# Issue order on ScalarE and VectorE in a two-layer hybrid block with eight routed experts

## The chip, the cores and the metric

The kernel runs on one core of a Trainium2 chip. The metric is device time in microseconds (us), median of several executions. TensorE (PE, its weight loads PEld), VectorE (DVE), ScalarE (ACT), GpSimd (POOL) and SyncE (SP) run side by side. Each takes its own instructions in the order in which the program was scheduled and waits on semaphores for the others. All weights are read from HBM by DMAs that SP issues.

## The reference

256 tokens of width 1024 go through two layers. A layer is a mixer (dilated attention, stick-breaking attention, a causal convolution, three gates, an output product) and a feed-forward part: a dense SwiGLU in layer 0, a routed one in layer 1. The change is in the routed one:

```python
logits = einsum(t, w_router) + b_router
top_logits, top_idx = lax.top_k(logits, 2)
gates = softmax(top_logits)
for each expert e, for the tokens routed to it:
    a = xb @ w_exp_gate[e]                  # 1024 x 2816
    u = xb @ w_exp_up[e]                    # 1024 x 2816
    y = (silu(a) * u) @ w_exp_down[e]       # 2816 x 1024
out[token] += gate * y
```

## The kernel before

**Precision.** Products run as pairs of fp32r operands: a value is `hi` (the value rounded by a ScalarE copy, L288) and `lo` (the rest, a VectorE subtraction, L292). A full expert does three products per weight tile (hi·hi, lo·hi, hi·lo).

**Experts.** The eight experts run in the order of `RANKS`, called E0 to E7 here. E0, E1, E3 and E5 are full (128 token slots, three products). E2, E4, E6 and E7 are short: 64 slots, the hi and lo halves of the tokens side by side in one stationary tile, so two products per weight tile, and a fold (L1198) of the lower half onto the upper after ScalarE has copied it out (`low`, L1195). In a short expert every fifth load (`WHOLE`) is not split: PE multiplies the raw fp32 tile. Each expert has 34 loads (E7 35), of 1 MB but for two (E7 four) of half that: 33 MB.

**The stream of weights.** `_Stream` makes units in order. `_make` issues the load of a unit into one of 9 load buffers (5 of `raw`, `MORE_BUFS` = 4 of `more`) and emits its `hi` and its `lo`, each into one of 8 part buffers, so that four split units fit. `next` hands out unit n and first fills the stream while no more than three split units wait (`AHEAD_E`): in the text of the program the split of unit n+3 stands ahead of the products of unit n.

**Stages of an expert.** Gate and up products by columns of 512 (`project_e`), two units each. At the end of a gate product ScalarE takes `silu` (`ea`, L1225); at the end of an up product VectorE multiplies (L1228). `turn` transposes the result on PE (`eaT`) and splits it into an `ehl` tile of the `slab` pool (4 KB per partition each, 8 of them; the gathered tokens `xg` take four of the pool for each pair of experts). Then the down products into two banks; `y_half` splits each half into `yhi` and `ylo`, and `scatter` multiplies by the transposed selection, ScalarE scales by the gate (`add`, L1155) and POOL adds into `x` (L1156). The last expert uses one VectorE instruction (L1158) in place of these two. Between the two experts of a pair (p odd) `gather` brings in the tokens of the next pair: four `piece`s, one to a tick, each two PSUM banks that ScalarE copies out (L1106).

**Ticks.** `tick()` runs after each unit's products. `later(n, fn)` puts `fn` n ticks on, so that small work goes between units.

**What sets the order.** The tile framework schedules each engine's instructions in an order of its own, from dependencies, the order in the text as priority, and its own estimate of when operands will be ready. `_InOrder` wraps an engine (`act_`, `dve_`) and ties each instruction behind the engine's previous one in the text. Before the change only the routing ahead of the experts uses these wrappers; in the experts ACT and DVE stand in the scheduler's order.

Of the kernel before, what the change touches and what calls it, by code (L numbers as in the profile page):

```python
# [7 lines left out]
F32 = mybir.dt.float32  # L8
# [25 lines left out]
RAW_BUFS = 5  # L34
PART_BUFS = 4
SLABS = 17
MORE_BUFS = 4
MORE_PARTS = 4
AHEAD = 3 * 1024
AHEAD_E = 3 * 2048  # L40
WARM = 7
MOE_SLABS = 8
UNIT_E = 2048
SHORT = P // 2

# [179 lines left out]
class _Stream:  # L225
# [3 lines left out]
    def __init__(self, tc, raw_pool, part_pool, ahead):  # L229
        self.tc = tc  # L230
        self.nc = tc.nc
        self.raw_pool = raw_pool
        self.part_pool = part_pool
        self.ahead = ahead
        self.plan = []
        self.units = []
        self.raws = {}
        self.more_pool = None
        self.more_parts = None
        self.hold = None  # L240
        self.lo_late = None
        self.turn = -1
        self.part_turn = -1
        self.made = 0
        self.waiting = 0

    def raw_tile(self, shape):

# [20 lines left out]
    def _make(self):  # L269
        nc = self.nc  # L270
        key, ci, u, ku, n, whole = self.units[self.made]
        size = ku * n
        self.made += 1
        src, length = self.plan[ci]
        if ci not in self.raws:
            raw = self.raw_tile([P, length])
            nc.sync.dma_start(raw, src() if callable(src) else src)
            self.raws = {ci: raw}
        part = self.raws[ci][:, u * size:(u + 1) * size]
        if whole:  # L280
            return key, 0, part.rearrange("p (k n) -> p k n", n=n), None
        self.waiting += size
        if 2 * size <= UNIT_E:
            both = self.part_tile("hilo")
            hi, lo = both[:, :size], both[:, size:2 * size]
        else:
            hi, lo = (self.part_tile(q)[:, :size] for q in ("hi", "lo"))
        ins = nc.scalar.activation(hi, part, AF.Copy)  # L288
        if self.lo_late is not None:
            self.tc.keep_in_program_order(ins)  # L290
        if self.lo_late is None:
            nc.vector.tensor_tensor(lo, part, hi.bitcast(F32), op=ALU.subtract)  # L292
        else:
            self.lo_late.append(lambda e: e.tensor_tensor(lo, part, hi.bitcast(F32), op=ALU.subtract))
        return (key, size, hi.rearrange("p (k n) -> p k n", n=n), lo.rearrange("p (k n) -> p k n", n=n))
# [34 lines left out]
def tile_kernel(ctx, tc, x, weights, experts, columns, consts, gains, out, dbg=None):  # L330
# [48 lines left out]
    for t in range(TT):  # L379
        nc.sync.dma_start(xs[t], x[0, t * P:(t + 1) * P, :])  # L380
    nc.scalar.dma_start(cols[:, :R_TAP], columns[:, :R_TAP])
    ident = con[:, C_ID:C_ID + P]
    ones = con[:, C_ONE:C_ONE + P]
    trir = cst.tile([P, P], F32R, name="trir")
# [653 lines left out]
        rt["slots"].append(sl)  # L1038

    def moe():  # L1040
        hhi, hlo, rs2, sels, picks, slots = (rt[k] for k in ("hi", "lo", "rs2", "sels", "picks", "slots"))

        low_1 = lambda e: low(1)
# [23 lines left out]
        def gather(pair, slots, at_once=False, late=()):  # L1067
# [25 lines left out]
            def piece(kp):  # L1093
                xg.append(T([P, 2, 2 * width], "xg", F32R))
                for j in range(2):
                    k = 2 * kp + j
                    b = ax_bank("xgp")
                    for q, src in enumerate((hhi, hlo)):
                        for t in range(TT):
                            pe.matmul(b[:, q * width:(q + 1) * width], src[:, t, k * P:(k + 1) * P],  # L1100
                                      slots_of[q][:, t], start=t == 0, stop=t == TT - 1)
                    to, of = xg[kp][:, j, :], b[:, :2 * width]
                    if both:
                        to = to.rearrange("p (i q s) -> p q i s", i=2, q=2)
                        of = of.rearrange("p (q i s) -> p q i s", i=2, q=2)
                    act.activation(to, of, AF.Copy)  # L1106

            pts, rss = [], []
            for fn in late:
# [35 lines left out]

        def scatter(gate, last, pt, yhi, ylo, h):
            sl = slice(h * 512, (h + 1) * 512)
            for t in range(TT):
                b = ax_bank("sc")
                pe.matmul(b, pt[:, t * P:(t + 1) * P], yhi[:, sl], start=True, stop=False)  # L1150
                pe.matmul(b, pt[:, t * P:(t + 1) * P], ylo[:, sl], start=False, stop=True)
                g = gate(t)
                if not last:
                    add = work.tile([P, 512], F32, tag="add", name="add", bufs=2)
                    act.activation(add, b, AF.Copy, scale=g)  # L1155
                    pool.tensor_tensor(xs[t][:, sl], xs[t][:, sl], add, op=ALU.add)  # L1156
                else:
                    dve.scalar_tensor_tensor(xs[t][:, sl], b, g, xs[t][:, sl], op0=ALU.mult, op1=ALU.add)  # L1158
            if last:
                later(1 if h else 4, lambda: store(sl))  # L1160

        def store(sl):
            for t in range(TT):
# [2 lines left out]
        def expert(i, short, part, pts, rss, gate, last, beside):  # L1166
# [74 lines left out]
            def y_half(h, bank):  # L1241
                sl = slice(h * 512, (h + 1) * 512)
                split_evac(yhi[:, sl], ylo[:, sl], bank)
                scatter(gate, last, pts[i], yhi, ylo, h)

            bk = [None, None]
            k_h = [0, 0]
# [163 lines left out]
```

## Time and profile before

| what | value |
|---|---|
| median of 3 executions | 1553.1 us (1551.66 to 1553.54) |
| profiled execution, its own time | 1553.46 us |
| its span in the trace | 1551.7 us |
| PE / PEld / DVE / ACT busy | 95% / 72% / 73% / 62% |
| granted TensorE clock | 0.989 |
| bytes moved by DMA | 400.17 MB |

The experts take from about 754 us to the end. The trace counts PE as busy while matmuls overlap, with modelled ends, so that a busy PE is not PE at its peak; the number of matmuls in a stretch and what they waited for tell more. "Idle before" of an engine names what released it.

### The profile page before, as it was taken

The page shows a single profiled execution, that of the slowest core. Times are in us where ns is not written, and L with a number is a line of the kernel's source. Part 1 is how long each engine was busy: PE and PEld are TensorE (multiplying, and loading weights), DVE is VectorE, ACT ScalarE, POOL GpSimd, SP SyncE. Part 2 cuts the span into 40 slices and gives each one's busy share as a digit, 9 for nine tenths or more (in the row PEclk, how much of TensorE's full clock was granted, in tenths as well). Part 3 has the DMA queues.
Part 4 walks back from the last instruction along what each step waited for, and adds up shares of the span by engine and source line. Part 5 has one row for each costly group of instructions (what it writes and reads, how often), then busy time and mean ns, then how long its engine had stood idle before and what let it go on. Part 6 is the DMA issues. An engine that isn't in the chain of part 4 may idle for free.

```text
span 1551.7 us, 17848 instructions
## 1 busy us (share of the span) xinstructions
PE 1480.0 (95%) x6596; PEld 1124.5 (72%) x6596; DVE 1132.7 (73%) x1233; ACT 967.5 (62%) x1039; POOL 92.8 (6%) x69
## 2 busy tenths in 40 slices
PE   9989999999999989999999999999998999989887
PEld 7867787788888777787888887557774577755554
DVE  5898657555547797666899887678875788677665
ACT  6646653544435656663877777667776677766664
POOL 0200000000000200000000202011010020100200
PEclk9999999999999999999999999999999999999999
DMA  8443344554555443447599988989898898898983
GB/s 350 138 167 130 132 162 173 185 184 173 185 190 180 146 163 109 151 175 285 219 378 376 362 312 327 366 340 364 326 371 330 339 372 335 341 340 320 384 312 122
DMA packets 57695, 400.17 MB, mean 258 GB/s; under 512 B 6528, under 2 KB 6784, under 8 KB 10752
## 3 DMA queue, kind: packets, MB, share of 16 engines
q1 hardware_dynamic: 57312, 398.85, 68.6%
q8 instruction: 54, 0.88, 0.2%
q14 instruction: 41, 0.34, 0.1%
q10 hardware_dynamic: 288, 0.10, 0.0%
HBM read 397.88 MB, written 1.05 MB: 257 GB/s over the span
## 4 chain that ended last, share of the span: by engine, by line
PE 70%; DVE 16%; ACT 7%; issue 4%; POOL 1%; DMA 0%; DVEq 0%; ACTq 0%; SPq 0%
PE ed L1183 13%; PE eg L1183 11%; PE eu L1183 9%; DVE lo L292 6%; ACT hi L288 5%; DVE acc L611 4%; DVE hilo L292 3%; PE gt L453 2%; PE gt L451 2%; PE gt L452 2%; POOL qkss L673 1%; PE fg L452 1%; PE fg L453 1%; PE fg L451 1%; PE fd L452 1%
## 5 line engine op out<-in xcount | busy, mean ns | idle before, releaser
L292 DVE TENSOR_TENSOR lo<-raw,hi 128x2048 fp32r<-128x2048 f32 x229 | 527.6, 2319 | 137.0 <-ACT hi L288 136.3
L288 ACT ACTIVATE hi<-raw 128x2048 fp32r<-128x2048 f32 x229 | 432.7, 1913 | 32.9 <-PE ed L1183 16.4
L292 DVE TENSOR_TENSOR hilo<-raw,hilo 128x1024 fp32r<-128x1024 f32 x240 | 290.4, 1221 | 178.3 <-ACT hilo L288 177.7
L288 ACT ACTIVATE hilo<-raw 128x1024 fp32r<-128x1024 f32 x244 | 254.0, 1059 | 231.8 <-PE fd L453 35.4
L1183 PE MATMUL eg<-hi,xg 128*128 128x512 f32 x528 | 142.6, 404 | 2.7 <-ACT hi L288 2.4
L1183 PE MATMUL eu<-hi,xg 128*128 128x512 f32 x448 | 119.1, 402 | 3.6 <-ACT hi L288 3.6
L1183 PEld LDWEIGHTS eg<-hi,xg 128*128 128x128 f32 x528 | 97.5, 190 | 30.4 <-ACT hi L288 8.4
L1183 PE MATMUL ed<-hi,ehl 128*128 128x512 f32 x444 | 117.6, 400 | 0.0
L1183 PE MATMUL eg<-lo,xg 128*128 128x512 f32 x344 | 98.3, 407 | 10.7 <-DVE lo L292 10.7
L1183 PEld LDWEIGHTS eu<-hi,xg 128*128 128x128 f32 x448 | 81.9, 188 | 29.9 <-ACT hi L288 9.8
L1183 PE MATMUL eu<-lo,xg 128*128 128x512 f32 x288 | 85.4, 418 | 15.5 <-DVE lo L292 15.5
L1156 POOL TENSOR_TENSOR x<-x,add 128x512 f32<-128x512 f32 x28 | 60.8, 2194 | 648.7 <-ACT add L1155 648.7
L611 DVE SCALAR_TENSOR_TENSOR acc<-uT,cols,acc 128x255 f32<-128x255 f32 (+29 forms) x240 | 97.0, 460 | 0.0
L1183 PEld LDWEIGHTS ed<-hi,ehl 128*128 128x128 f32 x444 | 81.4, 188 | 21.4 <-ACT hi L288 2.5
L1183 PE MATMUL ed<-lo,ehl 128*128 128x512 f32 x284 | 81.0, 407 | 6.0 <-DVE lo L292 5.6
L1183 PEld LDWEIGHTS eg<-lo,xg 128*128 128x128 f32 x344 | 62.1, 188 | 33.0 <-DVE lo L292 18.1
L1183 PEld LDWEIGHTS eu<-lo,xg 128*128 128x128 f32 x288 | 51.4, 190 | 39.2 <-DVE lo L292 28.0
L451 PE MATMUL gt<-hilo,hhi 128*128 128x512 f32 x192 | 76.9, 401 | 0.0
L453 PE MATMUL gt<-hilo,hhi 128*128 128x512 f32 x192 | 75.2, 391 | 0.0
L452 PE MATMUL gt<-hilo,hlo 128*128 128x512 f32 x192 | 75.1, 391 | 0.0
L1183 PEld LDWEIGHTS ed<-lo,ehl 128*128 128x128 f32 x284 | 52.2, 188 | 24.6 <-DVE lo L292 11.4
L513 ACT ACTIVATE ehl<-eaT 128x256 fp32r<-128x256 f32 (+2 forms) x48 | 22.2, 463 | 70.5 <-PE eaT L1209 57.9
(305 smaller groups left out, 2481.3 us busy)
## 6 DMA issues: line engine op xcount, KB each, us to landing
raw<-in_experts_dram SPq DMA_DIRECT2D x255, 1024.0 KB, 6.7
raw<-in_weights_dram SPq DMA_DIRECT2D x111, 1024.0 KB, 4.8
raw<-in_experts_dram SPq DMA_DIRECT2D x18, 512.0 KB, 5.4
raw<-in_weights_dram SPq DMA_DIRECT2D x4, 512.0 KB, 6.9
x<-in_x_dram SPq DMA_DIRECT2D x2, 512.0 KB, 4.3
out_dram<-x SPq DMA_DIRECT2D x4, 256.0 KB, 2.6
gain<-in_gains_dram SPq DMA_DIRECT2D x1, 512.0 KB, 3.8
att<-in_consts_dram SPq DMA_DIRECT2D x1, 448.0 KB, 7.0
```

The source lines that it names most:

```text
L288: ins = nc.scalar.activation(hi, part, AF.Copy)
L292: nc.vector.tensor_tensor(lo, part, hi.bitcast(F32), op=ALU.subtract)
L451: pe.matmul(dst, ahi, whi, start=first, stop=False)
L452: pe.matmul(dst, alo, whi, start=False, stop=False)
L453: pe.matmul(dst, ahi, wlo, start=False, stop=last)
L513: act.activation(hi, src, AF.Copy)
L611: dve.scalar_tensor_tensor(acc[:, c, lag:], uT[:, c, :S - lag], w, acc[:, c, lag:], op0=ALU.mult, op1=ALU.add)
L673: pool.tensor_tensor(ssf, ssf, half[:, :TT * 8], op=ALU.pow)
L1156: pool.tensor_tensor(xs[t][:, sl], xs[t][:, sl], add, op=ALU.add)
L1183: pe.matmul(b, a if wlo is not None else a.bitcast(F32), w[:, j, :], start=k0 + j == 0 and x == 0, stop=k0 + j == nk - 1 and x == len(todo ...
```

## The change

1. In `moe()` the names `act` and `dve` become the wrappers, and the stream's splits are tied in as well (`in_order`): every ScalarE and every VectorE instruction of the experts stands in the order of the text.
2. Results are taken some ticks later: the copies out of a `piece` one tick after its products, the scatter of a half one or two ticks after its split, its two `add`s one tick after the scatter. The last expert's scatter stays where it was, and so do the pieces of the first pair.
3. The `slab` pool has 10 tiles in the experts rather than 8; in the earlier stages the sum of `slab` and `slab2` stays 17.
4. `more` has 3 load buffers rather than 4: 8 in all.
5. A tile of 64 bytes in `small` that nothing uses, which moves all pools behind it.

```diff
-MORE_BUFS = 4
+MORE_BUFS = 3
-MOE_SLABS = 8
+MOE_SLABS = 10
...
+        self.in_order = False
...
         ins = nc.scalar.activation(hi, part, AF.Copy)
-        if self.lo_late is not None:
+        if self.lo_late is not None or self.in_order:
             self.tc.keep_in_program_order(ins)
         if self.lo_late is None:
-            nc.vector.tensor_tensor(lo, part, hi.bitcast(F32), op=ALU.subtract)
+            ins = nc.vector.tensor_tensor(lo, part, hi.bitcast(F32), op=ALU.subtract)
+            if self.in_order:
+                self.tc.keep_in_program_order(ins)
...
+    small.tile([P, 16], F32, tag="pad", name="pad_small", bufs=1)
...
     def moe():
+        nonlocal act, dve
+        act, dve, ws.in_order = act_, dve_, True
...
-                    to, of = xg[kp][:, j, :], b[:, :2 * width]
-                    if both:
...
-                    act.activation(to, of, AF.Copy)
+                    if at_once:
+                        taken(kp, j, b)
+                    else:
+                        later(1, lambda j=j, b=b: taken(kp, j, b))
...
         def scatter(gate, last, pt, yhi, ylo, h):
...
+                banks.append(b)
+                if last:
+                    dve.scalar_tensor_tensor(xs[t][:, sl], b, gate(t), xs[t][:, sl], op0=ALU.mult, op1=ALU.add)
             if last:
                 later(1 if h else 4, lambda: store(sl))
+            else:
+                later(1, lambda: added(gate, banks, sl))
+
+        def added(gate, banks, sl):
+            for t, b in enumerate(banks):
+                add = work.tile([P, 512], F32, tag="add", name="add", bufs=2)
+                act.activation(add, b, AF.Copy, scale=gate(t))
+                pool.tensor_tensor(xs[t][:, sl], xs[t][:, sl], add, op=ALU.add)
...
-                scatter(gate, last, pts[i], yhi, ylo, h)
+                if last:
+                    scatter(gate, last, pts[i], yhi, ylo, h)
+                else:
+                    later(1 + h, lambda: scatter(gate, last, pts[i], yhi, ylo, h))
```

## Rows read from the trace of the kernel before

**Rows 1.** Busy time by stretch, one expert each (E1 to E7), columns ahead.

```profile
core 0: us, PE busy (x) PEld busy (x) DVE busy (x) ACT busy (x) POOL busy (x), PEclk, DMA share, GB/s
...
850.10:949.30 99.20, 99.20 (x463) 81.49 (x462) 84.64 (x56) 74.56 (x62) 10.39 (x4) 1.00 0.92 344
949.30:1039.20 89.90, 84.91 (x299) 52.35 (x297) 59.55 (x38) 57.84 (x53) 8.53 (x4) 0.98 0.86 334
1039.20:1146.70 107.50, 105.44 (x476) 82.31 (x476) 93.59 (x59) 80.43 (x66) 10.78 (x4) 1.00 0.94 362
1146.70:1238.30 91.60, 83.78 (x298) 50.83 (x296) 60.06 (x37) 58.72 (x53) 5.90 (x4) 1.00 0.86 332
1238.30:1346.00 107.70, 105.67 (x476) 82.34 (x476) 90.95 (x54) 79.02 (x66) 10.77 (x4) 1.00 0.93 361
1346.00:1439.50 93.50, 84.18 (x299) 50.71 (x297) 61.42 (x38) 59.82 (x54) 5.34 (x4) 1.00 0.89 325
1439.50:1542.70 103.20, 90.31 (x311) 53.98 (x310) 70.03 (x46) 65.36 (x58) 9.11 (x4) 0.98 0.75 285
```

**Rows 2.** Waits of ACT in E2 to E7: for whom, us in total, times, longest.

```profile
ACT ehl L513 <- PE eaT L1209: 47.5, 21, 3.3
ACT low L1195 <- PE eg L1183: 42.4, 21, 3.7
ACT yhi L513 <- PE ed L1183: 36.1, 9, 7.4
ACT low L1195 <- PE eu L1183: 26.2, 18, 3.3
ACT ehl L513 <- PE ed L1183: 12.3, 6, 2.3
```

**Rows 3.** Waits of DVE in E2 to E7, the largest.

```profile
DVE lo L292 <- ACT hi L288: 119.1, 95, 5.3
```

**Rows 4.** Waits of all engines in E1, the largest of DVE.

```profile
DVE lo L292 <- ACT hi L288: 12.1, 18, 1.8
```

**Rows 5.** ACT in order of time, in E4.

```profile
1179.67 1.92 ACT L288 ACTIVATE hi<-raw 128x2048 fp32r<-128x2048 f32 x1
1185.25 0.59 ACT L1195 ACTIVATE low<-eg 64x512 fp32r<-64x512 f32 x1 [3.67 <-PE eg L1183]
1185.87 1.91 ACT L288 ACTIVATE hi<-raw 128x2048 fp32r<-128x2048 f32 x1
```

**Rows 6.** PE in the same stretch.

```profile
1181.56 3.60 PE L1183 MATMUL eg<-raw,xg 128*128 128x512 f32 x8
...
1190.16 1.20 PE L1183 MATMUL eu<-lo,xg 128*128 128x512 f32 x4 [1.13 <-DVE lo L292]
```

**Rows 7.** PE at the start of E4, where it waits for nothing.

```profile
1150.36 1.09 PE L1183 MATMUL eu<-hi,xg 128*128 128x512 f32 x4
1151.29 1.09 PE L1183 MATMUL eu<-lo,xg 128*128 128x512 f32 x4
1152.22 3.60 PE L1183 MATMUL eu<-raw,xg 128*128 128x512 f32 x8
1155.75 0.49 PE L1198 MATMUL eg<-low,fold 64*128 64x512 f32 x1
```

**Rows 8.** Readers of the load buffers in E2 to E7: min, median, max ns.

```profile
L288 ACT ACTIVATE hi<-raw x164: 1895/1908/1977, 948.2 to 1530.8; 128x2048 fp32r<-128x2048 f32 x164
L292 DVE TENSOR_TENSOR lo<-raw,hi x164: 2273/2292/3221, 950.1 to 1534.9; 128x2048 fp32r<-128x2048 f32 x164
```

**Rows 9.** Loads in E2 to E7: count, KB each, median us from issue to landing.

```profile
raw<-in_experts_dram SPq DMA_DIRECT2D x179, 1024.0 KB, 6.7
```

**Rows 10.** Busy time in two stretches in which the DMA engines had no pause.

```profile
1059.00:1072.00 13.00, 12.77 (x58) 9.93 (x57) 11.32 (x8) 9.41 (x7) 0.00 (x0) 1.00 0.99 373
...
1040.00:1054.00 14.00, 13.27 (x53) 9.45 (x54) 11.21 (x6) 12.35 (x12) 10.40 (x4) 1.00 1.01 421
```

**Rows 11.** DVE at the start of E0, one group of the small instructions of `count`.

```profile
L1314 DVE TENSOR_TENSOR prod<-one,slot 128x64 f32<-128x64 f32 x2 | 0.4, 218 | 0.0
```

More of the change, by code (lines that the diff above doesn't have):

```diff
@@ L1101, in piece, with taken @@
                                       slots_of[q][:, t], start=t == 0, stop=t == TT - 1)
-                    to, of = xg[kp][:, j, :], b[:, :2 * width]
-                    if both:
-                        to = to.rearrange("p (i q s) -> p q i s", i=2, q=2)
-                        of = of.rearrange("p (q i s) -> p q i s", i=2, q=2)
-                    act.activation(to, of, AF.Copy)
+                    if at_once:
+                        taken(kp, j, b)
+                    else:
+                        later(1, lambda j=j, b=b: taken(kp, j, b))
+            def taken(kp, j, b):
+                to, of = xg[kp][:, j, :], b[:, :2 * width]
+                if both:
+                    to = to.rearrange("p (i q s) -> p q i s", i=2, q=2)
+                    of = of.rearrange("p (q i s) -> p q i s", i=2, q=2)
+                act.activation(to, of, AF.Copy)
             pts, rss = [], []
@@ L1147, in scatter @@
             sl = slice(h * 512, (h + 1) * 512)
+            banks = []
             for t in range(TT):
@@ L1151, in scatter @@
                 pe.matmul(b, pt[:, t * P:(t + 1) * P], ylo[:, sl], start=False, stop=True)
[L1152 to L1158, printed above, removed]
+                banks.append(b)
+                if last:
+                    dve.scalar_tensor_tensor(xs[t][:, sl], b, gate(t), xs[t][:, sl], op0=ALU.mult, op1=ALU.add)
             if last:
                 later(1 if h else 4, lambda: store(sl))
+            else:
[5 more added lines that the diff above has]
+                pool.tensor_tensor(xs[t][:, sl], xs[t][:, sl], add, op=ALU.add)
         def store(sl):
```

## The prediction, made before the change was run

> **What bounds the kernel now.** I read first the busy time of PE expert by expert, then the waits of ACT and DVE in the bad stretches beside those in the good one, then one bad loop in order of time, and last the loads. In E1, PE does 463 matmuls in 99.2 us and is never counted idle; nothing holds it [rows 1]. E3 and E5 do the same work, with a few matmuls of their neighbours (476), in 107.5 and 107.7 us. The short experts have a third fewer matmuls (298 to 311) and still take 89.9, 91.6, 93.5 and 103.2 us [rows 1]. So six of eight experts are slower than their PE work.
>
> What they wait for: in E2 to E7 DVE's `lo` waited 119.1 us for `hi` [rows 3], in E1 12.1 us [rows 4], some 73 us for six experts of that kind. ACT, which makes `hi`, meanwhile stood in front of results that PE had not finished: 42.4 + 26.2 us before `low`, 36.1 before `yhi`, 47.5 + 12.3 before `ehl` [rows 2]. One loop shows it. After a `hi` at 1179.67 ACT waits 3.67 us for `low` and starts the next `hi` at 1185.87 [rows 5]. In that time PE is busy with a raw tile from 1181.56 on (3.60 us), then runs dry and waits 1.13 us for the `lo` of that late `hi` at 1190.16 [rows 6]. By then the split unit ahead of the raw tile was used up, so part buffers were free: `hi` was late only because `low` stood ahead of it in ACT's queue.
>
> Loads are not late. Nine buffers at 91.6/34 = 2.69 us a unit are 24.2 us for one round of a buffer; landing takes 6.7 us [rows 9], `hi` 1.91 and `lo` 2.29 [rows 8]; 13.3 us are left in which a loaded unit lies and waits. Engine time is no bound either: ACT is busy 57.8 us and DVE 59.6 of E2's 89.9 [rows 1].
>
> **The PE time of a short expert.** Unstalled, a split unit takes 1152.22 - 1150.36 = 1.86 us (eight matmuls of 0.2325), a raw one 1155.75 - 1152.22 = 3.53, a fold 0.49 [rows 7]. Counting halves, 26.5 split and 6.5 raw units and 11 folds are 49.3 + 22.9 + 5.4 = 77.6 us. For turns and scatter: E1's 33 units of twelve matmuls are 92.1 of its 99.2 us, so gather, turns and scatter are 7.1 there; I take 4 of it. Sum 81.6 us.
>
> **Program order (part 1).** In the text the `hi` and `lo` of unit n+3 stand ahead of unit n's products, and each result that ACT or DVE takes from unit n stands ahead of unit n+4's split, which can't start before PE has left unit n anyway (four units of part buffers). What it costs: when PE leaves unit n, ACT does `low` (0.6) or `ea` (0.7, behind a fold of 0.49), then `hi` 1.91, then DVE `lo` 2.29: 4.8 to 5.4 us. PE has three units left, 5.6 us, and needs `lo` only after the four `hi` matmuls, 0.93 us later: 6.5 us of cover. In a full expert the cover is 3 x 2.79 + 1.86 = 10.2 us. So the stall of [rows 5, 6] goes, and what is late next is PE's own work. Behind a waiting result on ACT stand the next `hi`s, behind one on DVE the next `lo`s, and PE waits for those; the margin is 1.1 us in a short expert without a raw unit in the window. At an expert's end `yhi` now stands behind the next expert's first three splits, so the dry start after each short expert goes too.
>
> Shorts E2, E4, E6: least 81.6, most what they take now. I take 85: 3.4 us for the four `add`s, whose POOL additions run beside `lo`s (a `lo` took 3.22 instead of 2.29 at worst, 0.93 x 4 = 3.7) [rows 8]. Gain 4.9 + 6.6 + 8.5 = 20.0. Full E3 and E5: 100.5, E1's 99.2 and 1.3 for the same; gain 7.0 + 7.2 = 14.2. E7: the 85 of a short, 2 for the last half, behind which nothing is left to cover `yhi`, `ylo` and the scatter, 3 for loads (below): 90, gain 13.2.
>
> E0 loses. `count` has 23 small DVE instructions of about 0.2 us [rows 11]; the scheduler spread them between `lo`s, in program order they stand in one block of some 4 us ahead of unit 4's `lo`, with DVE busy throughout (no idle time before that group). Least 0, most 4.6; I take 2.5.
>
> **Results in steps (part 2).** A tick is one unit, 1.9 to 2.8 us. The gathered tokens are needed ten units later and the sums in `x` only at the end, so the delay lies beside the down and gate products of PE; no DMA or SP instruction moves, and POOL's additions come a tick later on an engine that works 5 to 11 us in an expert [rows 1]. Four PSUM banks serve pieces, turns and scatters; were they short, PE would wait a tick (2.8 us) at a scatter or a piece, at most some 4 times in an expert of the three with a gather, 34 us in all; I take 0 because each bank is taken before the second next use. A gain of its own is excluded: the steps only keep part 1 from stalling.
>
> **Two slabs (part 3).** Four `xg` and six `ehl` of a pair's first expert need ten tiles; with eight, `ehl` waits for the down products to free one, 12.3 us on ACT [rows 2]. With ten this goes; it is inside the excess counted above. In the earlier stages the sum is the same: 0.
>
> **One load buffer less (part 4).** Eight buffers at 85/34 = 2.5 us are 20.0 us a round; less 6.7 + 4.2 a unit still lies 9.1 us; in a full expert (100.5/34) 12.7. A short expert's 34.6 million bytes take 82 to 93 us at the two rates that the trace shows with the DMA engines without a pause, 421 and 373 GB/s [rows 10]. So a short of 85 us eats 0 to 8 us of the 9.1, and a full one brings it back. E6 and E7 follow each other, hence the 3 us on E7. For the others 0, at most the DMA rival below.
>
> **The pad (part 5).** `hi` reads the buffers of two pools that lie at different places and has 1.895 to 1.977 us over 164 instances, `lo` takes 2.273 at least and 2.292 in the median [rows 8]; no place shows. 0, and 1 us either way.
>
> **The sum.** 20.0 + 14.2 + 13.2 - 2.5 = 44.9 us from the profiled execution's 1553.46: 1508.6. It lay 0.36 above the median of 1553.1, so 1508.2 us.
>
> **The rivals.**
> *The loads become the bound* (0.26). For it: DMA share is 0.86 to 0.94 already [rows 1], raw tiles hold their buffer until PE has used them, and a late load now blocks ACT with every result behind it, three units ahead of PE. Against: 9 us in hand. If nothing is in hand and the rate is the middle, 397 GB/s, a short takes 87.2 and E7 92.2: 13.4 + 14.2 + 11.0 - 2.5 = 36.1, 1517; at 373 GB/s 92.8 and 97: -3.4 + 14.2 + 6.2 - 2.5 = 14.5, 1538.6.
>
> *Nothing moves* (0.06): the loads can't go faster than they go in E3, 362 GB/s over the expert [rows 1]. With nothing in hand a short then takes 34.6 million bytes at 360 GB/s, 96 us, and E7 100: -13.0 + 14.2 + 3.2 - 2.5 = 1.9, 1551. Rows against: 421 GB/s over 14 us [rows 10]; and E3's PE is short of `lo`, not of loads. The Trainium skill, page "DMA: Bandwidth & Descriptors", section "Where 436 GB/s comes from", says that HBM to SBUF is bound at about 358 GB/s for a core, by which it would come out like this; the 421 of that stretch speaks against the rule here.
>
> *Slower: results block the splits* (0.14). In program order one late result stops all `hi`s behind it. A short expert has 12 results that need more PE work than the unit itself (six `ea` behind folds, six `ehl` behind transposes). PE's own order is still the scheduler's; where it puts the fold or the transposes one unit later than the text, ACT waits 1.86 (split) to 3.53 us (raw) more against a margin of 1.1, so PE stalls 0.8 to 2.4 us. At 12 x 1.5 = 18 us a short expert takes 99.6, and E2 to E7 take 4 x 99.6 + 2 x 99.2 + 2 = 598.8 against 593.4 now, with E0's 2.5: 1561. It decides from (97.6 - 81.6)/12 = 1.3 us a result, where the six experts take 590.9, and E0's 2.5 makes that 593.4. For it: `low` waited up to 3.67 us [rows 5]. Against: those waits come from `low` standing ahead of an older split, which the text never does.
>
> **How the numbers follow.** Forecast as summed, 1492 to 1517: 0.52; loads 1517 to 1540: 0.26; nothing 0.06; slower 0.14; all experts at PE's own time (1490 or less): 0.02. Range 1490 to 1550, from all costs at their least to the DMA rival with the pad and half of the case in which nothing moves; it leaves out the slower case. A measurement of this kernel can tell about 0.2% from no change; faster by more 0.80, within 0.06, slower 0.14.
>
> **What would show it.** Right: `hi` starts a unit's time after the last one throughout, ACT's waits before `low` stay but no longer end in a wait of PE for `lo`; E3 and E5 near 100 us, shorts near 85, DMA share over 0.95 in shorts. Wrong: `hi` waits on a landing (loads), or PE waits for `lo` right behind a fold or `eaT` (blocked results); E0 longer by more than 5 us; the stages ahead of 740 us changed by over 1 us, which would be the pad or the pools.

## The result and the profile after

The changed kernel takes 1532.75 us (median of three, 1531.95 to 1534.41) against 1553.1: a ratio of 0.9873, 95% interval 0.9859 to 0.9887. The profiled execution took 1531.95, its span 1530.2 us. The gain is 20.4 us; the forecast was 44.9.

Expert by expert, from the last down product of one to that of the next (worked out from both traces by the same bounds, so before differs from [rows 1] by a few us at the seams):

| | E0 | E1 | E2 | E3 | E4 | E5 | E6 | E7 |
|---|---|---|---|---|---|---|---|---|
| before | ends 847.3 | 100.2 | 91.5 | 105.9 | 93.3 | 106.0 | 95.2 | 102.5 |
| after | ends 849.2 | 102.1 | 89.5 | 104.1 | 87.8 | 103.7 | 89.5 | 94.8 |
| gain | -1.9 | -1.9 | 2.0 | 1.8 | 5.5 | 2.3 | 5.7 | 7.7 |
| forecast gain | -2.5 | 0 | 4.9 | 7.0 | 6.6 | 7.2 | 8.5 | 13.2 |

The gains sum to 21.2; with 0.3 behind the last product that is the difference of the spans, 21.5. Busy time of the same stretches of after, columns as in [rows 1]:

```profile
849.20:951.30 102.10, 100.73 (x467) 82.27 (x466) 85.07 (x55) 74.21 (x63) 10.69 (x4) 1.00 0.88 343
951.30:1040.80 89.50, 85.80 (x307) 54.15 (x305) 64.77 (x41) 63.33 (x57) 8.65 (x4) 0.98 0.88 347
1040.80:1144.90 104.10, 102.11 (x467) 81.99 (x466) 87.51 (x56) 75.16 (x63) 7.14 (x4) 1.00 0.93 367
1144.90:1232.70 87.80, 84.11 (x307) 53.44 (x305) 64.69 (x41) 63.47 (x57) 8.65 (x4) 1.00 0.90 356
...
1336.40:1425.90 89.50, 85.77 (x307) 54.05 (x305) 64.71 (x41) 63.22 (x56) 8.67 (x4) 0.98 0.87 346
1425.90:1520.70 94.80, 89.38 (x310) 55.25 (x308) 66.75 (x44) 59.72 (x55) 10.60 (x4) 0.96 0.80 322
```

E1, which was never idle, now is (100.73 busy of 102.10), and in E2, E6 and E7 the granted clock (third column from the right) is under 1. ACT's waits of after in E2 to E7, then DVE's:

```profile
ACT ehl L221 <- PE eaT L1227: 123.1, 33, 7.0
...
ACT low L221 <- PE eg L1201: 2.4, 3, 0.8
```
```profile
DVE lo L293 <- ACT hi L289: 75.4, 68, 5.1
DVE ehl L221 <- ACT ehl L221: 43.6, 26, 4.0
```

(What goes through the wrappers stands at their line, L221; `hi` and `lo`, tied in as well, keep L289 and L293. The lines of the changed kernel lie 1 to 18 further down than those of [rows].) The waits before `low` are gone, as foreseen: 42.4 + 26.2 us in [rows 2], 2.4 now. DVE's `lo` waits 75.4 in place of 119.1 [rows 3]. But ACT now stands 123.1 us before `ehl`, where it stood 47.5 [rows 2]. One such place, the start of E2's down products in after, first ACT, then DVE, then PE (start, duration, operation, idle before it and what ended that):

```profile
1004.55 0.59 ACT L221 ACTIVATE low<-eg 64x512 fp32r<-64x512 f32 x1
1010.06 0.38 ACT L221 ACTIVATE ehl<-eaT 128x256 fp32r<-128x256 f32 x1 [4.92 <-PE eaT L1227]
1010.34 1.90 ACT L289 ACTIVATE hi<-raw 128x2048 fp32r<-128x2048 f32 x1
```
```profile
1002.75 4.49 DVE L293 TENSOR_TENSOR lo<-raw,hi 128x2048 fp32r<-128x2048 f32 x2 [0.83 <-ACT hi L289]
1007.16 0.74 DVE L221 SCALAR_TENSOR_TENSOR ea<-eu,rss,ea 64x512 f32<-64x512 f32 x1
```
```profile
1003.49 0.49 PE L1216 MATMUL eu<-low,fold 64*128 64x512 f32 x1
...
1009.56 0.46 PE L1227 MATMUL eaT<-con,ea 64*128 64x64 f32 x4
1012.29 0.97 PE L1201 MATMUL ed<-hi,ehl 128*128 128x512 f32 x3 [2.27 <-ACT hi L289]
...
1014.23 3.23 PE L1201 MATMUL ed<-raw,ehl 128*128 128x512 f32 x4
...
1018.23 1.88 PE L1201 MATMUL ed<-raw,ehl 128*128 128x512 f32 x4
```

PE's fold ends `eu` at 1003.98. DVE could multiply then, but in the text `ea` stands behind two `lo`: it starts at 1007.16, 3.18 us late. PE does the transposes in its own order at 1009.56, ACT's `ehl` follows, and only then the next `hi`, which is done at 1012.24. From the fold's end that is 8.26 us. PE had 6.04 us of work, the transposes last, and then ran dry for 2.27.

The two `lo` were late themselves. Their `hi`s stood on ACT behind the `ehl` of the chunk before, for which ACT had waited:

```profile
997.41 0.39 ACT L221 ACTIVATE ehl<-eaT 128x256 fp32r<-128x256 f32 x1 [2.95 <-PE eaT L1227]
```

So the chain closes on itself: a late `ehl` makes `hi` and `lo` late, and these the next `ea`.

The dry spot has a second price. The granted clock of after around it:

```profile
1008.00:1012.00 4.00, 2.02 (x11) 1.34 (x10) 0.42 (x1) 1.94 (x2) 0.00 (x0) 1.00 1.01 424
1012.00:1018.00 6.00, 5.71 (x13) 3.01 (x14) 4.90 (x3) 5.90 (x7) 0.00 (x0) 0.72 0.84 321
1018.00:1024.00 6.00, 6.00 (x22) 3.86 (x21) 4.74 (x3) 1.72 (x1) 0.00 (x0) 1.00 0.61 214
```

After 4 us with PE half busy it is 0.72 over 6 us, a stretch between the full 2.4 GHz and the lower 1.2, and four raw matmuls take 3.23 us, where they take 1.88 at full clock. In E6 and E7 the clock falls as well (0.98 and 0.96 over the expert). E4 has the same dry spot, but a clock of 1.00 throughout: its down products take 26.9 us, those of E2 and E6 28.5. So the clock costs 1.6 us in E2 and in E6.

### The profile page after: what moved, and what is told of

Same layout as the page of the kernel before. It is cut to its first block, busy times and chain, and to the rows that moved or that the text cites. A ratio compares the mean times of both kernels' runs of the same rounds, so it can differ in the third digit from the quotient of the medians.

```text
span 1530.2 us, 17821 instructions
## 1 busy us (share of the span) xinstructions
PE 1473.0 (96%) x6596; PEld 1132.0 (74%) x6596; DVE 1131.6 (74%) x1233; ACT 961.1 (63%) x1039; POOL 93.5 (6%) x69
## 3 DMA queue, kind: packets, MB, share of 16 engines
q1 hardware_dynamic: 57312, 398.85, 68.2%
## 4 chain that ended last, share of the span: by engine, by line
PE 75%; DVE 13%; ACT 6%; issue 3%; POOL 1%; DMA 0%; ACTq 0%; SPq 0%; DVEq 0%
PE eg L1201 14%; PE ed L1201 14%; PE eu L1201 10%; DVE acc L616 4%; ACT hi L289 4%; DVE hilo L293 3%; DVE lo L293 3%; PE gt L458 2%; PE gt L456 2%; PE gt L457 2%; POOL qkss L678 1%; PE fg L457 1%; PE fg L458 1%; PE fg L456 1%; PE fd L457 1%
## 5 line engine op out<-in xcount | busy, mean ns | idle before, releaser
L293 DVE TENSOR_TENSOR lo<-raw,hi 128x2048 fp32r<-128x2048 f32 x229 | 525.3, 2312 | 104.5 <-ACT hi L289 94.2
L289 ACT ACTIVATE hi<-raw 128x2048 fp32r<-128x2048 f32 x229 | 431.5, 1913 | 21.4 <-PE ed L1201 12.9
L293 DVE TENSOR_TENSOR hilo<-raw,hilo 128x1024 fp32r<-128x1024 f32 x240 | 290.6, 1221 | 176.6 <-ACT hilo L289 176.0
L289 ACT ACTIVATE hilo<-raw 128x1024 fp32r<-128x1024 f32 x244 | 254.3, 1059 | 229.7 <-PE fd L458 35.2
L1201 PE MATMUL ed<-hi,ehl 128*128 128x512 f32 x444 | 123.6, 409 | 10.3 <-ACT hi L289 10.0
L1201 PE MATMUL eu<-hi,xg 128*128 128x512 f32 x448 | 125.0, 408 | 0.9 <-ACT hi L289 0.9
L221 ACT ACTIVATE ehl<-eaT 128x256 fp32r<-128x256 f32 (+2 forms) x48 | 22.2, 463 | 162.0 <-PE eaT L1227 162.0
L1201 PE MATMUL eu<-lo,xg 128*128 128x512 f32 x288 | 81.0, 401 | 2.0 <-DVE lo L293 2.0
L1201 PEld LDWEIGHTS eg<-lo,xg 128*128 128x128 f32 x344 | 63.4, 188 | 25.4 <-DVE lo L293 10.7
```

The lines of the kernel that those rows point to most:

```text
L221: return self.tc.keep_in_program_order(getattr(self.engine, name)(*args, **kw))
L293: ins = nc.vector.tensor_tensor(lo, part, hi.bitcast(F32), op=ALU.subtract)
L1201: pe.matmul(b, a if wlo is not None else a.bitcast(F32), w[:, j, :], start=k0 + j == 0 and x == 0, stop=k0 + j == nk - 1 and x == len(todo ...
```

## The experiments

Each ran beside the kernel before on the same chip; ratios are to that kernel.

| kernel | median us | ratio, 95% interval |
|---|---|---|
| 1 changed, without program order | 1556.7 | 1.0027 [1.0018, 1.0037] |
| 2 before, eight load buffers | 1555.4 | 1.0018 [1.0008, 1.0027] |
| 3 changed, PE in program order too | 1530.6 | 0.9848 [0.9829, 0.9867] |
| 4 changed, splits of a turn a tick later | 1497.7 | 0.9648 [0.9632, 0.9664] |
| 5 changed, eight slabs, nine loads | 1534.6 | 0.9883 [0.9864, 0.9902] |
| 6 changed, without steps | 1562.6 | 1.0063 [1.0040, 1.0086] |
| 7 changed, splits two ticks later | 1498.8 | 0.9651 [0.9635, 0.9667] |
| 8 as 4, count and end moved | 1493.8 | 0.9621 [0.9605, 0.9637] |
| 9 changed, whole turn a tick later | 1498.5 | 0.9651 [0.9635, 0.9667] |
| 10 before, program order alone | 1568.0 | 1.0107 [1.0079, 1.0134] |
| 11 changed, without the pad | 1533.2 | 0.9886 [0.9863, 0.9908] |
| 12 as 3, turn and splits later | 1496.6 | 0.9642 [0.9626, 0.9658] |
| 13 changed, `ehl` out of the order | 1534.4 | 0.9887 [0.9871, 0.9904] |
| 14 changed, `ea` on DVE out of the order | 1502.1 | 0.9684 [0.9668, 0.9700] |
| 15 as 12, with the moves of 8 | 1496.9 | 0.9637 [0.9621, 0.9653] |

### What each part is worth (1, 2, 5, 6, 10, 11)

**Without program order:**

```diff
-        act, dve, ws.in_order = act_, dve_, True
+        act, dve, ws.in_order = act, dve, False
```


> The changed kernel with the scheduler's order on ScalarE and VectorE again; the results in steps, the ten slabs, the eight load buffers and the pad stay. Theory (program order makes the whole gain, the rest is worth nothing by itself): 1550 to 1556 us, like the kernel before, and DVE's wait of lo for hi in the experts is back at some 119 us. Rival A (the steps or the slabs make a gain of their own, by taking results out of ACT's way): under 1546 us. Rival B (the load buffer that was given up costs time, and program order made more than the 20.4 us that the comparison shows): over 1557 us, with hi waiting for landings at the starts of E3, E5 and E7.

1556.7 us, 0.7 above the range of the theory and just short of rival B's: the rest of the change without program order loses 4 us, and in E2 to E7 `lo` waits 114.4 us for `hi` again.

**Eight load buffers in the kernel before:**

```diff
-MORE_BUFS = 4
+MORE_BUFS = 3
```


> The kernel before with one load buffer less, eight in all, and nothing else of the change. Theory (loads lay loaded 9 to 13 us before hi took them, so a buffer less is hidden): 1552 to 1555 us. Rival (at the starts of the full experts E3 and E5 and of E7 the raw tiles of the short expert ahead hold their buffers until PE has used them, and one buffer less makes hi wait there): 1556 to 1565 us, and this part then explains 3 to 12 of the 24.5 us by which the changed kernel fell short of the forecast.

1555.4, at the edge of the two: in the kernel before the buffer's loss costs some 2.8 us, most of the 4 above. But not in E3, E5 and E7, where the rival put it (105.9, 106.0 and 101.3 us against 105.9, 106.0 and 102.5); E0 to E2 and E4 got longer by about 1 us each, in a traced execution of 1557.2 us, the longest of the ten.

**Eight slabs and nine loads in the changed kernel:**

```diff
-MORE_BUFS = 3
+MORE_BUFS = 4
...
-MOE_SLABS = 10
+MOE_SLABS = 8
```


> The changed kernel with eight slabs and nine load buffers, as the kernel before had them: parts 3 and 4 of the change undone together, since the memory of a core holds only one of the two. Theory (under program order the two slabs are needed: in E2, E4 and E6 the last two ehl of an expert stand ahead of four hi and wait for the down products to free a slab, where the scheduler let the hi go first): 1536 to 1548 us, and a wait of ehl for ed, as the kernel before has it, comes back with more than 12.3 us. Rival (the load buffer is worth more than the slabs: in the changed kernel hi waits for landings 6.6 us at the starts of E3, E5 and E7): 1525 to 1531 us.

1534.6; 1532.75 lies inside its runs (1531.9 to 1537.3), so neither account decides. The traces say more. The slabs are missed in E0 alone, whose down products take 37.9 us in place of 30.6, behind this wait of ACT in them:

```profile
ACT ehl L221 <- PE ed L1201: 13.4, 2, 9.1
```

E2 is 2.6 us shorter, E1 1.7; whether by the ninth buffer or by loads that got ahead while E0 stood, this kernel can't tell, since it changes both. E3, E5 and E7 take 104.0, 103.7 and 94.9 us with nine load buffers, 104.1, 103.7 and 94.8 with eight: in the changed kernel the load buffer is worth nothing there.

**Without the steps** (pieces, scatters and `add` taken at once):

```diff
-                        later(1, lambda j=j, b=b: taken(kp, j, b))
+                        taken(kp, j, b)
...
-                later(1, lambda: added(gate, banks, sl))
+                added(gate, banks, sl)
...
-                    later(1 + h, lambda: scatter(gate, last, pts[i], yhi, ylo, h))
+                    scatter(gate, last, pts[i], yhi, ylo, h)
```


> The changed kernel without the steps: pieces, scatters and add are taken in the tick of their products, as in the kernel before; program order, slabs, loads and pad stay. Theory (part 2 is worth nothing by itself, but in program order a result taken at once stands ahead of the next hi until PE has done its products, as ehl does in the changed kernel): three gathers and seven scatters cost 1 to 3 us each, 1538 to 1555 us, and ACT's waits for xgp and sc grow. Rival (the steps change nothing, since PE does a piece or a scatter within the margin): 1530 to 1535 us.

1562.6 us: the steps are worth 29.9 us in program order. Place of it: not the pieces (ACT waits 0.9 us for `xgp`) but `add`. ACT at the start of E3 without the steps:

```profile
1047.12 0.58 ACT L221 ACTIVATE yhi<-ed 128x512 fp32r<-128x512 f32 x1
1057.62 1.27 ACT L221 ACTIVATE add<-sc,gr 128x512 f32<-128x512 f32 x2 [9.92 <-PE sc L1162]
1058.77 1.91 ACT L289 ACTIVATE hi<-raw 128x2048 fp32r<-128x2048 f32 x1
```

One result stops every `hi` for 9.92 us; in the gate and up products of E2 to E7 PE waits 25.4 us for `hi` (14.4 in `eg`, 11.0 in `eu`; 0.9 in the changed kernel).

**Program order alone**, on the kernel before (with `in_order` in the stream as in the change):

```diff
     def moe():
+        nonlocal act, dve
+        act, dve, ws.in_order = act_, dve_, True
```


> The kernel before with program order on ScalarE and VectorE and nothing else of the change (no steps, eight slabs, nine load buffers, no pad). The changed kernel without the steps took 1562.6 us. Theory (program order alone loses, since every result that is taken in the tick of its products stops the splits; the steps then make 30 us, and slabs and loads little): 1557 to 1575 us. Rival (the eight load buffers and not the missing steps made that loss): 1540 to 1553 us.

1568.0 us (1563.9 to 1571.9), as the theory has it: the same edit that, with the steps and the slabs, makes the gain loses 14.7 us without them. Part of that is the slabs': E0's down products take 37.8 us here, much as in 5, and 30.6 in kernel 6, which lacks the steps alone and loses 10.1. **Without the pad:**

```diff
-    small.tile([P, 16], F32, tag="pad", name="pad_small", bufs=1)
```


> The changed kernel without the tile of 64 bytes. Theory (no place in memory shows in the durations of hi and lo): 1531 to 1535 us, hi and lo at 1.91 and 2.31 us on average. Rival (the pad moves the part buffers to better places): lo over 2.36 us on average and 1537 us or more.

1533.2 us, `lo` at 2.313 us on average against 2.312. The pad is worth nothing.

### Why the gain is half (3, 4, 7, 9, 13, 14)

**PE in program order too:**

```diff
-        nonlocal act, dve
+        nonlocal act, dve, pe
         act, dve, ws.in_order = act_, dve_, True
+        pe = pe_
```


> The changed kernel with PE's instructions of the experts in program order too. In the changed kernel ACT stands 162 us before ehl, and PE does the transposes eaT some three units later than the text has them; behind ehl stand the next four hi, behind upped the next lo. Theory (PE's own order blocks the results, and with them the splits): the wait before ehl falls under 90 us, the dry 2.27 us at the start of the down products of E2, E4, E6 and E7 goes, with the lower clock behind it, and the time is 1515 to 1526 us. Rival (the results are late because their chain is long, whatever PE's order is; in text order PE itself then stands before ea and waits, with matmuls behind it that could run): 1533 to 1560 us.

1530.6 us. The wait before `ehl` fell from 162.0 to 75.5 us, as the theory says, and the time hardly moved. That is two things against each other: E1 to E7 are 8.1 us shorter, but E0 ends 8.2 us later (its first gate product starts 3.2 us later, and PE waits 3.6 us before its first transposes). PE's largest wait in E2 to E7 of this kernel:

```profile
PE eaT L221 <- DVE ea L221: 14.9, 12, 1.8
```

In the text the transposes of E2, E4 and E6 stand two to three units ahead of where the scheduler had put them on PE. Moved there, PE itself stands before them and waits for `ea`. So PE's own order was not the cause alone; this was the first pointer at DVE.

**Splits of a turn a tick later:**

```diff
-                src = b[:, :nf * ns].rearrange("p (f s) -> p f s", s=ns)
+                later(1, lambda: turned_out(c0, b, nf))
+
+            def turned_out(c0, b, nf):
+                src = b[:, :nf * ns].rearrange("p (f s) -> p f s", s=ns)
```


> The changed kernel with the splits of a turned chunk (ehl, L221) put one tick after its transposes, so that in the text one more hi and lo stand ahead of them. Theory (ehl stands ahead of four hi that could run, and a tick brings PE's transposes in time): the wait before ehl falls from 162 to some 100 us, the dry spots of 2.27 us in E2, E4, E6 and E7 shrink, with some 2 us of lower clock in three of them: 1520 to 1528 us. Rival (the chain ehl, four hi, lo, product, transposes, ehl closes on itself and a tick only moves the place of the wait): 1531 to 1537 us.

1497.7 us: 35 us better than the changed kernel, and far past the theory's 1520 to 1528, which counted the dry spots alone. PE's idle time in E1 to E7 falls by 19.9 us; the other 15 are busy time for as many matmuls (649.8 us, now 634.7), part of it the clock in E2, E6 and E7. E2 to E5, and E7:

```profile
949.10:1032.30 83.20, 83.20 (x307) 53.74 (x305) 64.40 (x41) 61.80 (x56) 8.67 (x4) 1.00 0.92 368
1032.30:1132.50 100.20, 100.20 (x468) 82.39 (x467) 87.82 (x56) 76.99 (x64) 7.14 (x4) 1.00 0.98 385
1132.50:1215.70 83.20, 83.20 (x307) 53.73 (x305) 64.37 (x41) 62.85 (x56) 8.68 (x4) 1.00 0.93 374
1215.70:1316.00 100.30, 100.30 (x468) 82.40 (x467) 87.67 (x56) 75.22 (x64) 7.14 (x4) 1.00 0.96 383
...
1399.20:1485.60 86.40, 84.63 (x310) 54.19 (x308) 66.79 (x44) 61.48 (x56) 10.58 (x4) 1.00 0.87 356
```

PE is busy throughout E2 to E6 and the clock is 1.00. The prediction had 85, 100.5, 85, 100.5 and 90. ACT waits for landings more than in the changed kernel (12.7 us against 6.6), and PE for none of it. **Two ticks:**

```diff
-                later(1, lambda: turned_out(c0, b, nf))
+                later(2, lambda: turned_out(c0, b, nf))
```


> The changed kernel with the splits of a turned chunk two ticks after its transposes; one tick gave 1497.7 us, with 83.2 us for each of E2, E4 and E6, 100.2 for E3 and E5, and no wait of PE but one of 1.8 us. Theory (what was missing was the order alone, and one tick is past the point from which it decides: what is left is PE's own work): 1495 to 1500 us, the shorts within 0.5 us of 83.2. Rival A (a wait of 52.8 us before ehl is left, so a second tick gains again): under 1495 us. Rival B (with two ticks the last ehl of an expert come too late for the down products, or a bank is held too long): over 1500 us.

1498.8, as the theory has it: the wait before `ehl` falls from 52.8 to 11.9 us, and nothing is gained. **The whole turn, transposes and splits, a tick later**, in the changed kernel:

```diff
-                    later(1, lambda: turn(c0, a))
+                    later(2, lambda: turn(c0, a))
```


> The changed kernel with the whole turn of a chunk, transposes and splits, two ticks after the product on VectorE in place of one. The splits stand right behind the transposes in the text, as in the changed kernel; only the room between the product and the transposes grows. Theory (ACT waits because the result is asked for in the tick of its own products, so moving both leaves the wait where it was): 1527 to 1536 us, the wait before ehl stays over 100 us in E2 to E7. Rival (the transposes came late because the product on VectorE came late, behind older lo, and the room between product and transposes is what was short): 1495 to 1515 us.

1498.5: my theory fell, the time is the rival's. The wait before `ehl` is 54.4 us in E2 to E7, with `ehl` as close behind its transposes as ever. But by the traces this is kernel 4 over again: from E1 on ACT and DVE have the same order in both, and in the shorts PE does the transposes at the same places, so the room between `ea` and the transposes did not grow there. What grew, in both, is the room between `ea` and `ehl`. Two accounts were left, and two kernels were to tell them apart: `ehl` out of program order (13), and only `ea` on DVE out of it (14).

```diff
+            def freely(hi, lo, src):
+                nc.scalar.activation(hi, src, AF.Copy)
+                nc.vector.tensor_tensor(lo, src, hi.bitcast(F32), op=ALU.subtract)
...
-                    split_evac(hl[:, :, :SHORT], hl[:, :, SHORT:], src)
+                    freely(hl[:, :, :SHORT], hl[:, :, SHORT:], src)
...
-                    split_evac(hl[:, 0], hl[:, 1], src)
+                    freely(hl[:, 0], hl[:, 1], src)
```


> The changed kernel with the splits of a turned chunk (ehl on ScalarE and VectorE) alone out of program order, in the scheduler's place; ticks as in the changed kernel. Account A (ehl stands too early in ScalarE's queue, and everything else follows from that): 1495 to 1510 us, if the scheduler lets a hi or two go ahead of it. Account B (the product ea on VectorE is late and with it the transposes; ehl only shows it): 1522 to 1535 us. A third way (out of the order, ehl stands at worse places, as in the kernel before, with 70.5 us of waits before it): over 1535 us.

```diff
-                    dve.scalar_tensor_tensor(a[rows], bu[rows, :n], r1(), a[rows], op0=ALU.mult, op1=ALU.mult)
+                    nc.vector.scalar_tensor_tensor(a[rows], bu[rows, :n], r1(), a[rows], op0=ALU.mult, op1=ALU.mult)
```


> The changed kernel with the product on VectorE at the end of an up product (ea, line 1246) alone out of program order, in the scheduler's place; ticks as in the changed kernel. In the changed kernel it starts 4.5 us later than PE's last product, behind two lo. Account B (it is this product that makes the transposes late): 1495 to 1512 us, with the transposes some 4 us earlier and the wait before ehl under 90 us. Account A (ehl stands too early in ScalarE's queue, and a VectorE product that is earlier by less than a tick leaves that so): 1522 to 1537 us.

Kernel 13 takes 1534.4 us, with 124.6 us of waits before `ehl`, and is no test of account A. The scheduler left the freed `ehl` where the text had them: counted in the traces, 44 of the 48 stand behind as many weight splits as in the changed kernel, on ACT and on DVE, and the other four one split earlier. At the place shown above:

```profile
1012.11 0.38 ACT L1224 ACTIVATE ehl<-eaT 128x256 fp32r<-128x256 f32 x1 [4.91 <-PE eaT L1231]
```

Freeing the one DVE instruction (14) gives 1502.1. The same place, E2's last chunks, in that trace, DVE then PE:

```profile
999.91 0.74 DVE L1246 SCALAR_TENSOR_TENSOR ea<-eu,rss,ea 64x512 f32<-64x512 f32 x1 [3.41 <-PE eu L1216]
1000.58 4.48 DVE L293 TENSOR_TENSOR lo<-raw,hi 128x2048 fp32r<-128x2048 f32 x2
```
```profile
999.31 0.49 PE L1216 MATMUL eu<-low,fold 64*128 64x512 f32 x1
...
1000.08 1.09 PE L1201 MATMUL eu<-lo,xg 128*128 128x512 f32 x4
1001.10 0.27 PE L1227 MATMUL eaT<-con,ea 64*128 64x64 f32 x1
```

`ea` starts 0.11 us after the fold's end in place of 3.18, and the transposes begin 1.30 us after that end in place of 5.58. So not `ea` alone moved: PE's order is the scheduler's, and it put the transposes of the shorts up to three units earlier as well. All 48 `ehl` stand on ACT where they stood.

Kernel 4 moved the other end. All 48 `ea` stand there behind as many `lo` as in the changed kernel, and in the shorts the transposes stand on PE where they stood, within one matmul; 44 of the 48 `ehl` stand one split later. The same place in its trace, DVE, ACT, then PE:

```profile
999.85 0.74 DVE L221 SCALAR_TENSOR_TENSOR ea<-eu,rss,ea 64x512 f32<-64x512 f32 x1
1005.88 0.39 ACT L221 ACTIVATE ehl<-eaT 128x256 fp32r<-128x256 f32 x1 [1.30 <-PE eaT L1227]
```
```profile
999.31 0.49 PE L1216 MATMUL eu<-low,fold 64*128 64x512 f32 x1
...
1005.38 0.46 PE L1227 MATMUL eaT<-con,ea 64*128 64x64 f32 x4
1005.77 0.50 PE L1201 MATMUL ed<-hi,ehl 128*128 128x512 f32 x1
```

Behind the same two `lo`, `ea` starts 0.05 us after the fold's end, since no `ehl` held these `lo` up. The transposes begin 5.58 us after that end, as late as in the changed kernel, and yet PE does not run dry: the `hi` that it needs next was made ahead of `ehl`.

So neither account holds alone, and `ea`'s place is not the one cause. What the runs show is the closed chain: the text asks for `ehl` one tick after `ea`, and until `ehl` is done no `hi` behind it can start. The chain opens when `ehl` stands a split later (4, 9) and when `ea` and the transposes come earlier (14); with the transposes alone in text order it does not (3).

### Better than both (8, 12, 15)

**The count and the end**, on kernel 4: the count's DVE instructions in the scheduler's order, the last expert's additions to `x` (now in `added`) a tick after the scatter.

```diff
         def count():
+            dve = nc.vector
...
-            if last:
-                later(1 if h else 4, lambda: store(sl))
-            else:
-                later(1, lambda: added(gate, banks, sl))
+            later(1, lambda: added(gate, banks, sl, last))
+            if last:
+                later(2 if h else 5, lambda: store(sl))
```


> The kernel with the splits one tick later (1497.7 us), with the instructions of the count on VectorE in the scheduler's order again, and the last expert's additions to x one tick after the scatter's products, so that the splits of the last weights don't stand behind them. Theory (the block of the count costs 2.2 us in E0, and the additions cost 1.8 us before hilo in E7): 1492.5 to 1495 us, E0's gate and up products 66 us in place of 68.2, and no wait of PE for hilo. Rival (the block only moves, and a tick at the end of the last expert is added to the tail behind PE's last product): 1497 to 1500 us.

1493.8 us, the best time here. E0's gate and up products take 66.8 us (68.2 in the changed kernel, 65.8 before), E7 84.4:

```profile
1398.50:1482.80 84.30, 84.30 (x310) 54.19 (x308) 66.71 (x44) 61.59 (x56) 10.55 (x4) 1.00 0.89 368
```

**PE in program order with room everywhere** (12: kernel 3 with 4 and 9):

```diff
+        pe = pe_
...
-                    later(1, lambda: turn(c0, a))
+                    later(2, lambda: turn(c0, a))
...
+                later(1, lambda: turned_out(c0, b, nf))
```


> The changed kernel with PE in program order too, the transposes two ticks after the product on VectorE and the splits one tick after the transposes. PE in program order alone took 1530.6 us and stood 4 us in each short expert before the transposes, for ea of DVE. Theory (what decides is that each result is asked for at least a tick after its work could be done; whether the order is the text's or the scheduler's is second): 1495 to 1502 us. Rival (PE in the text's order has waits of its own that no tick takes away, or the third tick makes the first down products wait): 1510 to 1530 us.

1496.6 us, as the theory has it. Its shorts are the fastest of all, at a DMA rate over the whole expert that the kernel before reached in none [rows 1]:

```profile
949.50:1029.80 80.30, 80.30 (x307) 53.12 (x305) 66.52 (x42) 63.43 (x57) 10.17 (x4) 1.00 0.94 385
...
1392.80:1483.90 91.10, 85.80 (x311) 55.51 (x309) 64.08 (x43) 59.23 (x55) 10.22 (x4) 0.96 0.82 336
```

The shorts E2, E4 and E6 gain 9.1 us over kernel 4's and the whole only 1.1: E7 takes 90.9 us (86.4 there), E5 1.8 more, E1 and E3 1.0 together. **With the moves of 8** (15; the edit against 12, beside that of 8):

```diff
-                    later(2, lambda: turn(c0, a))
+                    later(1 if last else 2, lambda: turn(c0, a))
...
                 if last:
-                    scatter(gate, last, pts[i], yhi, ylo, h)
+                    later(1, lambda: scatter(gate, last, pts[i], yhi, ylo, h))
                 else:
-                    later(1 + h, lambda: scatter(gate, last, pts[i], yhi, ylo, h))
+                    later(2 + h, lambda: scatter(gate, last, pts[i], yhi, ylo, h))
```


> The kernel with PE in program order too, transposes two ticks after the product and splits one tick after them (1496.6 us; its short experts took 80.1 to 80.3 us, 3 less than with the scheduler's order on PE, but E7 90.9), with the count in the scheduler's order, the last expert's transposes one tick after the product, its scatter and additions a tick later each, and the other scatters a tick later. Theory (2 us from E0, as measured, and 4 to 6 of E7's 90.9 us, where PE waited 2.1 us for the first ehl, and 3.7 us before the scatter of the expert ahead): 1487 to 1491 us, better than 1493.8. Rival (the loads, which hi already waited 15.6 us for, give the gain back): 1492 to 1497 us.

15 was to mend E7 and missed: 1496.9 us, with E7 at 94.3, 10 us above kernel 8's. Six of these are PE idle: its transposes, at one tick again, made PE wait 4.3 us for `ea`, kernel 3's lesson once more, and it waits 1.7 us before a scatter. Four are busy time for as many matmuls, at a lower clock. In E7's gate and up products the DMA engines are busy throughout, in 15 (first) as in kernel 8:

```profile
1392.30:1455.70 63.40, 59.34 (x211) 37.12 (x209) 45.10 (x28) 46.28 (x43) 8.35 (x4) 0.97 1.00 413
```
```profile
1398.50:1455.70 57.20, 57.20 (x211) 36.55 (x209) 45.81 (x27) 45.30 (x42) 10.55 (x4) 1.00 1.01 420
```

Since PE is never idle in the second, a busy DMA does not show that the loads are the limit, as the rival of 15 has it. `hi` waits for one landing at the start of 15's E7, 3.8 us; how much of the 10 us comes from that stays open.

## Why the prediction was wrong

What bounds the kernel was read rightly: PE's own work is the limit, `hi` was late because older results stood ahead of it, and loads had time in hand. Once nothing stands ahead of the splits, E2 to E7 take what the sum said or less, and kernel 4 lies 10.5 us under the forecast. But the change moved the block in place of removing it, and the prediction's own sign of blocked results came true: PE runs dry right behind `eaT`, though for `hi`, not for `lo`. The DMA share in the shorts was to be over 0.95 and is 0.80 to 0.90.

| gain, us | E0 | E1 | E2, E4, E6 | E3, E5 | E7 | sum |
|---|---|---|---|---|---|---|
| forecast | -2.5 | 0 | 20.0 | 14.2 | 13.2 | 44.9 |
| after | -1.9 | -1.9 | 13.2 | 4.1 | 7.7 | 21.2 |
| kernel 4 | -1.8 | 0.2 | 30.4 | 11.4 | 16.1 | 56.3 |

**The step that failed is the margin of part 1.** It set a need of 4.8 to 5.4 us against a cover of 6.5. The need was that of one result on ACT, one `hi` and one `lo`, begun when PE leaves the unit. For `low` this holds: its waits are gone. `ehl` was left out of it, and `ehl` is not ready then, as `ea` on DVE and the transposes on PE come first. At the place shown that is 3.18 us of `ea` behind two late `lo`, 0.74 of `ea`, 1.66 until PE comes to the transposes, 0.46 for them: 6.04 us, in which PE uses up the three units that the sum gave it (5.6). Then come `ehl` and the `hi` behind it, which end 8.26 us after the fold, with nothing left to cover them: 2.22 us, the dry spot of 2.27. The prediction asked what stands behind a result on DVE and on ACT. It did not follow a result through all its engines, nor ask what stands ahead of it on each. With `ehl` a split later (4) 35.1 us come back, with `ea` freed and the transposes earlier (14) 30.6.

**Full experts.** E1, E3 and E5 were to have 10.2 us of cover and nothing to pay. E1 and E3 took 2 us more in their down products, E5 1.6, where the next pair's gather runs (37.7 us in E1 and E3, 35.7 in kernel 4): a `piece` of PE waits for a bank that DVE's `ehl` holds, 3.3 us over three such waits in E1 to E7, so some 1.1 us in each. Part 2 of the prediction had put the wait for a bank at 0. With the tick it is gone. E3 and E5, which follow a short, lost another 1.9 in their gate and up products (66.6 us, 64.7 in kernel 4).

**E7.** Against kernel 4 its gate and up products and its down products take 4.2 us more each, by the same chain and a clock of 0.96. The 3 us for loads were not needed: with eight buffers E7 takes 86.4 there. The 2 us for the last half were right in size by luck: they stood for a half that nothing covers, and what E7 has is 1.8 us of wait for `hilo` behind the additions to `x`, which kernel 8 gets back.

**The slower rival named the mechanism, at a wrong place and price.** Results block the splits, by `ehl`, as it said, and the scheduler does put the transposes later on PE than the text; but that is not enough: with text order on PE (3) they wait for `ea`, E1 to E7 gain 8.1 us of some 35, and E0 loses as much. Its price, 18 us in a short expert, was 89.5 - 83.2 = 6.3 in E2 and E6, so the sign stayed. Its 0.14 and the forecast's 0.52 had no case between them: the same block at a third of the price was missing, and where the time came out, 1517 to 1540, stood the loads with 0.26, for which PE is not seen to wait in the changed kernel.

**The other parts.** Steps at 0 was right only as part of the change: they are what keeps program order from losing (6, 10), and this was said without a price; it is some 30 us. Without program order the slabs show no gain (1); with it, going without them costs 7.3 us in E0's down products (5), which the prediction did not price. The pad was rightly put at nothing (11). The load buffer at nothing holds in E3, E5 and E7 of the changed kernel (5); in the kernel before it costs 2.8 us (2). E0's block was right: 1.9 for 2.5, and 1.4 of its 2.4 in the gate and up products came back with the count freed (8).

**Nothing moves**, the rival that the loads can't go faster than E3's 362 GB/s [rows 1], is out: E2 of kernel 12 moves 385 GB/s over 80 us, and E3 of kernel 4 as much over 100. The Trainium skill, page "DMA: Bandwidth & Descriptors", section "Where 436 GB/s comes from", has about 358 GB/s as the bound from HBM to SBUF for a core; the trace does not agree.

## What to carry to other kernels

Before tying instructions into program order, follow each result through every queue that it passes, add what stands ahead of it on each, and hold the sum against the work that the bounding engine has until then. A result should be asked for a tick or more after its work can be done: with the same order, one tick more room made 35 us here, and taking the ticks away lost 30. A long wait on an engine with slack is a pointer, not a cost: the second tick took 40.9 us of the waits before `ehl` away and gained nothing (7). And an edit that only frees an instruction has tested nothing until the order is seen to change: the scheduler left the freed `ehl` in place (13), and with the freed `ea` it moved the transposes too (14).

## What the hardware showed beside that

A dry spot of TensorE cost more than its length: after 4 us with PE busy 2.02 us the granted clock was 0.72 over the next 6 us in E2, and 1.00 again after that; against E4, which has the dry spot and not the lower clock, that is 1.6 us on top of 2.27. It does not follow each time, and what decides it stays open. And the loads kept up 385 GB/s over a short expert (12) and 413 and 420 over 63 and 57 us (15, 8), where the trace of before had such rates only in the short stretches of [rows 10].
